# A decoder layer on one core: the mean-square matmul one block later with the next weight halves ahead of the normalisation, the last projection in 256 columns, the norm weight ahead of the scaling

## The chip, the cores and the metric

One Trainium2 chip, one of its cores. A core has a matrix engine (PE, with PEld for its weight loads), a vector engine (DVE), a scalar engine (ACT), GpSimd (POOL) and a sync engine (SP) that here issues nearly all DMAs. Each engine runs its own instructions in the order in which the program holds them, and waits for the others through semaphores. The metric is the device time of one execution in microseconds; lower is better.

## The reference

A decoder layer on 256 tokens of width 1024: a first SwiGLU feed-forward block, a mixer (a Mamba-2 branch beside a retention branch), a second feed-forward block, and a final norm. Nine vectors computed from a conditioning vector shift, scale and gate the three blocks. All is float32. Cut to what the change touches:

```python
def modulate(x, shift, scale):
    return x * (1.0 + scale[:, None, :]) + shift[:, None, :]

def swiglu(x, w_in, w_out):
    gate, up = jnp.split(x @ w_in, 2, axis=-1)
    return (jax.nn.silu(gate) * up) @ w_out

u = modulate(rms_norm(h, norm_ffn1_w[l]), sh1, sc1)
h = h + 0.5 * g1[:, None, :] * swiglu(u, ffn1_w_in[l], ffn1_w_out[l])
u = modulate(rms_norm(h, norm_mix_w[l]), sh2, sc2)
h = h + g2[:, None, :] * hybrid_mixer(u, ...)      # starts with u @ mix_w_in
u = modulate(rms_norm(h, norm_ffn2_w[l]), sh3, sc3)
h = h + 0.5 * g3[:, None, :] * swiglu(u, ffn2_w_in[l], ffn2_w_out[l])
return rms_norm(h, norm_final_w)
```

## The kernel before

Activations lie transposed, features on the partitions and the 256 tokens (`T`) along the row. Each float32 matrix product is done as three fast matmuls: both operands are split into a high half (rounded, float32r) and a low half (the rest), and `mm3` adds high x high, high x low and low x high into one bank (lines 143 to 151). Weights come by DMA in tiles of 2048 words (`wst`, four buffers). `half` turns 1024 words of one into a pair (`wh`, four buffers): ACT casts the high half, DVE subtracts it to get the low half. `HALVES_AT` says at which words of the buffer the two halves start. `pair_project` is the usual projection: a load, two such conversions, 48 matmuls of 256 columns with the weights stationary and u (tiles `uh` and `ul`) moving.

At two places, ahead of the mixer and ahead of the second feed-forward block, `modulated` hides the normalisation. The residual step leaves the unnormalised, scaled tiles in `nT` (or `s`) and in u. `early_project` projects these into four banks, in eight blocks of 12 matmuls (one for each of the eight feature tiles, `kt`), with two extra columns that carry the shift, so 258 columns. Between the blocks stands the mean-square matmul of `rstd` (line 217, two float32 matmuls of two passes each). ACT and DVE turn its result into the factor `rs`, then, for each of the eight tiles, DVE multiplies by `rs` (line 263), ACT writes the high half of the true u (line 234) and DVE the low half (line 235). Each u tile may only be overwritten when its early block is done. At the end the early banks are scaled by `rs` (lines 267 and 268).

What follows differs. In the mixer it is the dt tile, 16 short matmuls with a weight tile of its own (`dt_tile`: its halves are split by lines 140 and 141), then `conv.8`, a `pair_project` at columns `C_XS + 8 * 256`. In the second feed-forward block it is the gate half of the second pair, a `pair_project` at column 256. Nothing in these parts has an order written out by hand: a scheduler puts each engine's instructions into one order when the program is built, from its own estimate of when each could run.

The last projection (`ffn2_w_out`) is turned round: activations are stationary (`ah`, `al`), weights move. It runs over three blocks of output columns, 512, 256 and 256 wide; in each, for every one of 22 feature tiles and two row tiles, three matmuls. Behind each block come the gate (`gb`), the residual (`hN`), a square with its sum (`ss`) for the final norm and, but for the last block, the norm weight (`wf`). Behind the last, for each row tile, a square root, a reciprocal, the scaling and the DMAs to the output.

Of the kernel before, what the change touches and what calls it, by code (L numbers as in the profile page):

```python
# [12 lines left out]
F32 = mybir.dt.float32  # L13
# [5 lines left out]
P = 128  # L19
# [17 lines left out]
N_VEC = 344  # L37

U_ROW = 320
HALVES_AT = {"still": (6, 1056), "alike": (48, 1072), "moved": (26, 1088)}  # L40

K_ID, K_TRI, K_M = 0, 128, 256
K_INV, K_SGN = 384, 385
# [37 lines left out]
def layer(ctx: ExitStack, tc: tile.TileContext, a, out, packing):  # L81
# [71 lines left out]
    def at(pair, *idx):  # L153
        return pair[0][idx], pair[1][idx]
# [99 lines left out]
        dve.scalar_tensor_tensor(am, modc[:, jsc, :], 1.0, col[:, vn:vn + KD], ALU.add, ALU.mult)  # L254
        return am

    def modulated(ha, u, jsh, w, cols):
        rs = []
        ps = early_project(w, cols, u, 1, lambda: rs.append(rstd(sums, mean_m)))
        rs = rs[0]  # L260
        for f in range(KD):
            t = ha(f)
            dve.tensor_tensor(t, t, rs, ALU.mult)
            u_tile(u, f, t, jsh)
        b = sp.tile([P, 4], F32, tag="eb", name=nm("eb"), bufs=1)
        for i in range(4):
            dve.tensor_copy(b[:, i:i + 1], ps[i][:, T:T + 1])
            dve.tensor_tensor(ps[i][:, :T], ps[i][:, :T], rs, ALU.mult)
        return [(ps[i][:, :T], b[:, i:i + 1]) for i in range(4)]

    def early_project(w, cols, u, at_kt, between):
        sts = [load(w, 0, KD, c0, 256) for c0 in cols]
# [209 lines left out]
    with tc.tile_pool(name=nm("fp"), bufs=1, reuse_waits="tile") as fp:  # L482
# [41 lines left out]
        while ada_todo[0][0] in (2, 4):  # L524
# [1 line left out]
        am = scale_col(V_N2, 4)  # L526
        contract("ffn1_w_out", NF, lambda kt: (ah[:, kt, :], alo[:, kt, :]),
                 residual(2, 0.5, am, lambda f: nT[:, f, :], u, 3), lambda: ada_next(3, 5))
        first = modulated(lambda f: nT[:, f, :], u, 3, "mix_w_in", (C_Z, C_Z + 256))
    with tc.tile_pool(name="mx", bufs=1, reuse_waits="tile") as mx:  # L530
        def slot(shape, dt=F32, name="s"):
            return mx.tile(shape, dt, tag="slot", name=nm(name), bufs=SLOTS)
# [15 lines left out]
        rows = dp.tile([2, NH, P], F32, name="rows")  # L548

        def conv_pair(f0, dst):  # L550
            ps = pair_project(w_in, C_XS + f0 * P, u)
            t = mx.tile([P, 2, T], F32, tag="cv", name=nm("cv"), bufs=2)
            for f in range(2):
                def wc(tap):
                    i = V_CW + tap * 24 + f0 + f
                    return col[:, i:i + 1]
                act.activation(t[:, f, :], ps[:, f, :], AF.Identity,
                               bias=col[:, V_CB + f0 + f:V_CB + f0 + f + 1], scale=wc(3))
                for sh in (1, 2, 3):
                    dve.scalar_tensor_tensor(t[:, f, sh:], ps[:, f, :T - sh], wc(3 - sh),  # L560
                                             t[:, f, sh:], ALU.mult, ALU.add)
            lookup(dst, t, AF.Silu)
# [376 lines left out]
        def ha(f):  # L939
            return hA[f // 4][:, f % 4, :]  # L940
        contract("mix_w_out", 8, lambda kt: at(mh[kt // 4], al, kt % 4),
                 residual(5, 1.0, am, ha, u, 6), lambda: ada_next(6))
        first = modulated(ha, u, 6, "ffn2_w_in", (0, FFN))
    table("silu_and_others")
    with tc.tile_pool(name=nm("fp"), bufs=1, reuse_waits="tile") as fp:
        ah, alo = (fp.tile([P, NF * T + n], F32R, name=nm(name))[:, n:]
                   .rearrange("p (f t) -> p f t", f=NF) for name, n in (("ah", 0), ("al", 0)))
        w1 = "ffn2_w_in"
        hN = fp.tile([P, 2, D], F32, name="hN")
        gb = fp.tile([P, D], F32, name="gb")  # L950
# [1 line left out]
        for p2 in range(NF // 2):  # L952
            if p2 == 0:
                s = fp.tile([P, 2, T], F32, tag="s", name=nm("s"), bufs=2)
                for f in range(2):
                    lookup(s[:, f, :], first[f][0], AF.Silu, bias=first[f][1])
                    dve.scalar_tensor_tensor(s[:, f, :], first[2 + f][0], first[2 + f][1],
                                             s[:, f, :], ALU.add, ALU.mult)
                split_into(ah[:, 0:2, :], alo[:, 0:2, :], s)
            else:  # L960
                pg = pair_project(w1, p2 * 256, u)
                pu = pair_project(w1, FFN + p2 * 256, u)
                swiglu(fp, pg, pu, ah, alo, 2 * p2)
            ada_next()
            if p2 == 1:
                nc.sync.dma_start(wf, a["norm_final_w"].broadcast_to([P, D]))
            if p2 == 5:
                g = sp.tile([P, KD], F32, tag="g", name=nm("g"), bufs=2)
                dve.tensor_scalar(g, modc[:, 8, :], 0.5, None, ALU.mult)
                diag = fp.tile([P, KD, P], F32, tag="diag", name="diag")  # L970
                dve.tensor_tensor(diag, ident.unsqueeze(1).broadcast_to([P, KD, P]),
                                  g.unsqueeze(2).broadcast_to([P, KD, P]), ALU.mult)
                for q in range(2):
                    ps = misc_ps()
                    pe.matmul(ps, ones, diag[:, 4 * q:4 * q + 4, :].rearrange("p f t -> p (f t)"),  # L975
                              start=True, stop=True)
                    act.copy(gb[:, q * 512:(q + 1) * 512], ps)
            if p2 == 6:
                for tt in range(2):
                    for q in range(2):  # L980
                        ps = misc_ps()
                        for f in range(4):
                            pe.transpose(ps[:, f * P:(f + 1) * P],  # L983
                                         h[:, q * 4 + f, tt * P:(tt + 1) * P], ident)
                        act.copy(hN[:, tt, q * 512:(q + 1) * 512], ps)
# [3 lines left out]
        for bi, (c0, n) in enumerate(blocks):  # L989
# [4 lines left out]
            for k0 in range(0, NF, per):  # L994
                kn = min(per, NF - k0)
                st = load("ffn2_w_out", k0 * P, kn, c0, n)
                hvs = [half(st[:, k2:min(k2 + per // 2, kn), :],
                            "moved" if n == 256 else "alike") for k2 in range(0, kn, per // 2)]
                order = [(kk, tt) for kk in range(kn) for tt in range(2)]
                if final and k0 + kn == NF:  # L1000
                    order = [(kk, tt) for tt in range(2) for kk in range(kn)]
                for kk, tt in order:
                    kt, ts = k0 + kk, slice(tt * P, (tt + 1) * P)
                    mm3(ps[tt], (ah[:, kt, ts], alo[:, kt, ts]),
                        at(hvs[kk // (per // 2)], al, kk % (per // 2)), kt == 0, kt == NF - 1,
                        turned=n == 256 and tt == 0 and kt % 4 == 2)
            for tt in range(2):
                t = fp.tile([P, 512], F32, tag="t", name=nm("t"), bufs=2)[:, :n]
                o = hN[:, tt, cs_]
                dve.tensor_tensor(t, ps[tt], gb[:, cs_], ALU.mult)  # L1010
                dve.tensor_tensor(o, o, t, ALU.add)
                act.activation(t, o, AF.Square, accum_out=ss[:, tt, bi:bi + 1])
                if not final:
                    dve.tensor_tensor(o, o, wf[:, cs_], ALU.mult)
                if bi == 1:
                    s3 = ss[:, tt, 3:4]
                    dve.tensor_tensor(s3, ss[:, tt, 0:1], ss[:, tt, 1:2], ALU.add)
# [1 line left out]
                if final:  # L1019
# [1 line left out]
                    lookup(r, r, AF.Sqrt, bias=ss[:, tt, 3:4], scale=1.0 / D)  # L1021
                    dve.reciprocal(r, r)
                    rows = slice(tt * P, (tt + 1) * P)
                    lo_, mid = hN[:, tt, :512], hN[:, tt, 512:768]
                    if tt == 0:
                        act.activation(mid, mid, AF.Copy, scale=r)
                    else:
                        dve.tensor_scalar(mid, mid, r, None, ALU.mult)
                    dve.scalar_tensor_tensor(o, o, r, wf[:, cs_], ALU.mult, ALU.mult)
                    nc.sync.dma_start(out[rows, 512:], hN[:, tt, 512:])  # L1030
                    act.activation(lo_, lo_, AF.Copy, scale=r)
                    (act if tt else nc.sync).dma_start(out[rows, :512], lo_)


_SHAPES = {
# [39 lines left out]
```

## Time and profile before

| | us |
|---|---|
| three timed runs | 836.59, 839.97, 839.66 (median 839.66) |
| the profiled execution | 839.59 |
| its span in the trace | 836.8 |
| mean granted clock of PE | 0.998 of full speed |
| busy ACT, DVE | 515.6, 664.5 |

The page gives for each engine its busy time and share of the span, and lists of waits with what released them. A row of the timeline has a start in us from the span's start, the length in us, the engine, the line of the program, the operation, what it writes and reads, and how many such instructions in a row it stands for. On PE a matmul's end is modelled, so its pace is read from starts.

### The profile page before, as it was taken

What the parts mean: (1) busy time and instruction counts of PE and PEld (TensorE: products, weight loads), DVE (VectorE), ACT (ScalarE), POOL (GpSimd) and SP (SyncE); (2) the same over time, 40 slices, a digit from 0 to 9 for tenths busy, and PEclk for the clock granted to TensorE, in tenths of its full rate; (3) what the DMA queues carried; (4) which work ended last, traced back from release to release, by engine and by line L of the source; (5) the groups of instructions that cost most, each with busy time, mean ns of one, the idle gap of its engine ahead of it and who ended that gap; (6) DMA issues with size and microseconds to landing.
All of it is one profiled execution on the core that took longest, in us unless ns stands there. A gap on an engine that the chain in (4) does not pass through costs nothing. (4 is left out here: it accounts for less than half of the span.)

```text
span 836.8 us, 16156 instructions
## 1 busy us (share of the span) xinstructions
PE 821.9 (98%) x6734; PEld 795.6 (95%) x6734; DVE 664.5 (79%) x1002; ACT 515.6 (62%) x743; POOL 10.3 (1%) x21
## 2 busy tenths in 40 slices
PE   7999999999999999999999999999999999999996
PEld 6999999999999989999999999999999999999896
DVE  5999879896989987788898778977979985455463
ACT  6665444365888687756565569765658654545342
POOL 0000000000110010000000000000000000000000
PEclk9999999999999999999999999999999999999999
DMA  9987779995595555546658664655555785455521
GB/s 365 413 349 271 289 291 331 340 363 193 186 319 202 201 201 179 180 159 227 219 197 302 235 219 151 207 197 169 221 198 200 264 334 197 156 202 176 188 89 50
DMA packets 30586, 193.13 MB, mean 231 GB/s; under 512 B 3489, under 2 KB 4129, under 8 KB 10034
## 3 DMA queue, kind: packets, MB, share of 16 engines
q1 hardware_dynamic: 28656, 186.40, 61.0%
q0 software_dynamic: 1568, 5.28, 2.0%
q8 instruction: 52, 0.85, 0.4%
q10 hardware_dynamic: 290, 0.44, 0.1%
q14 instruction: 20, 0.16, 0.0%
HBM read 191.02 MB, written 1.08 MB: 230 GB/s over the span
## 5 line engine op out<-in xcount | busy, mean ns | idle before, releaser
L136 DVE TENSOR_TENSOR wh<-wst,wh 128x1024 fp32r<-128x1024 f32 (+1 forms) x263 | 316.6, 1208 | 103.7 <-ACT wh L135 102.7
L135 ACT CAST wh<-wst 128x1024 fp32r<-128x1024 f32 (+1 forms) x263 | 271.8, 1038 | 169.2 <-PE proj L151 115.3
L149 PE MATMUL proj<-uh,wh 128*128 128x256 f32 (+1 forms) x1160 | 322.2, 278 | 0.0
L150 PE MATMUL proj<-ul,wh 128*128 128x256 f32 (+1 forms) x1160 | 321.7, 277 | 0.0
L151 PE MATMUL proj<-uh,wh 128*128 128x256 f32 (+1 forms) x1160 | 321.3, 277 | 0.0
L150 PEld LDWEIGHTS proj<-ul,wh 128*128 128x128 f32 x1160 | 217.8, 188 | 0.9 <-issue 0.2
L151 PEld LDWEIGHTS proj<-uh,wh 128*128 128x128 f32 x1160 | 217.8, 188 | 0.5 <-DVE wh L404 0.2
L149 PEld LDWEIGHTS proj<-uh,wh 128*128 128x128 f32 x1160 | 217.9, 188 | 0.3 <-ACT wh L135 0.2
L149 PE MATMUL proj<-s,wh 128*128 128x256 f32 x312 | 86.9, 280 | 0.3 <-ACT s L140 0.3
L150 PE MATMUL proj<-s,wh 128*128 128x256 f32 x312 | 86.3, 277 | 0.0
L151 PE MATMUL proj<-s,wh 128*128 128x256 f32 x312 | 86.2, 277 | 0.0
L193 DVE SCALAR_TENSOR_TENSOR wst<-wst,cb 128x1024 f32<-128x1024 f32 x56 | 67.1, 1220 | 9.7 <-DMA wst<-in_ada_w_dram 9.2
L149 PEld LDWEIGHTS proj<-s,wh 128*128 128x128 f32 x312 | 58.4, 188 | 0.7 <-ACT s L140 0.5
L150 PEld LDWEIGHTS proj<-s,wh 128*128 128x128 f32 x312 | 58.5, 188 | 0.3 <-issue 0.2
L151 PEld LDWEIGHTS proj<-s,wh 128*128 128x128 f32 x312 | 58.6, 188 | 0.0
L151 PE MATMUL proj<-ah,wh 128*128 128x256 f32 x152 | 42.5, 279 | 1.6 <-DVE wh L136 1.6
L149 PE MATMUL proj<-ah,wh 128*128 128x256 f32 x152 | 42.1, 277 | 0.0
L150 PE MATMUL proj<-al,wh 128*128 128x256 f32 x152 | 42.0, 276 | 0.0
L145 PE MATMUL proj<-uh,wh 128*128 128x256 f32 x152 | 42.0, 276 | 0.0
L146 PE MATMUL proj<-uh,wh 128*128 128x256 f32 x152 | 42.0, 276 | 0.0
L147 PE MATMUL proj<-ul,wh 128*128 128x256 f32 x152 | 42.0, 276 | 0.0
L173 ACT ACT_TABLE_LOAD x30 | 38.5, 1283 | 1.2 <-PEq L1048 0.7
(271 smaller groups left out, 1370.2 us busy)
## 6 DMA issues: line engine op xcount, KB each, us to landing
wst<-in_mix_w_in_dram SPq DMA_DIRECT2D x52, 1024.0 KB, 4.9
wst<-in_ffn_w_in_dram SPq DMA_DIRECT2D x43, 1024.0 KB, 5.5
wst<-in_ada_w_dram SPq DMA_DIRECT2D x28, 1024.0 KB, 6.2
wst<-in_ffn_w_out_dram SPq DMA_DIRECT2D x17, 1024.0 KB, 5.5
ada<-in_ada_w_dram SPq DMA_DIRECT2D x16, 512.0 KB, 12.5
wst<-in_w_br_ssd_dram SPq DMA_DIRECT2D x8, 1024.0 KB, 5.5
wst<-in_w_br_ret_dram SPq DMA_DIRECT2D x8, 1024.0 KB, 4.8
wst<-in_ffn_w_out_dram SPq DMA_DIRECT2D x6, 768.0 KB, 5.9
```

Of the source, the lines that this page charges most:

```text
L135: act.copy(hi, v)
L136: dve.tensor_tensor(lo, v, hi.bitcast(F32), ALU.subtract)
L145: pe.matmul(o, l[1], r[0], start=False, stop=False, skip_group_check=skip)
L146: pe.matmul(o, l[0], r[0], start=False, stop=False, skip_group_check=skip)
L147: pe.matmul(o, l[0], r[1], start=False, stop=False, skip_group_check=skip)
L149: pe.matmul(o, l[0], r[0], start=first, stop=False, skip_group_check=skip)
L150: pe.matmul(o, l[0], r[1], start=False, stop=False, skip_group_check=skip)
L151: pe.matmul(o, l[1], r[0], start=False, stop=last, skip_group_check=skip)
L173: ins = act.preload_act_table_set(name).ins
L193: dve.scalar_tensor_tensor(st[:, i, :], st[:, i, :], 1.0, cb, ALU.mult, ALU.mult, accum_out=raw[:, j, f0 + i:f0 + i + 1])
```

## The change

Three parts.

1. `modulated` calls `rstd` ahead of the third block of the early projection and not of the second. Behind it, and ahead of the normalisation, it now loads and converts the weights of the next projection (`pair_halves`), and hands the two pairs to `conv.8` or to the second pair of the feed-forward block, which no longer make them.
2. In the last projection the 512-wide block is done as two matmuls of 256 columns each into the two parts of the bank. All three blocks use the same places for the halves, with the low half at word 1050, 1024 behind the high one. The tile of the low activations begins 26 words (104 bytes) later.
3. The norm weight is multiplied in at once for every block, ahead of the square root and the reciprocal; the square is written to a tile of its own. Behind the last block the first row tile is scaled in one piece of 1024 columns and goes out in one DMA of 512 KB; the second is scaled in two pieces of 512.

```diff
-HALVES_AT = {"still": (6, 1056), "alike": (48, 1072), "moved": (26, 1088)}
+HALVES_AT = {"still": (6, 1056), "alike": (48, 1072), "moved": (26, 1050)}
...
-    def modulated(ha, u, jsh, w, cols):
+    def modulated(ha, u, jsh, w, cols, c_next):
         rs = []
-        ps = early_project(w, cols, u, 1, lambda: rs.append(rstd(sums, mean_m)))
+        ps = early_project(w, cols, u, 2, lambda: rs.append(rstd(sums, mean_m)))
         rs = rs[0]
+        ready = pair_halves(w, c_next)
         for f in range(KD):
             t = ha(f)
             dve.tensor_tensor(t, t, rs, ALU.mult)
...
-        return [(ps[i][:, :T], b[:, i:i + 1]) for i in range(4)]
+        return [(ps[i][:, :T], b[:, i:i + 1]) for i in range(4)], ready
...
-        first = modulated(lambda f: nT[:, f, :], u, 3, "mix_w_in", (C_Z, C_Z + 256))
+        first, ready = modulated(lambda f: nT[:, f, :], u, 3, "mix_w_in", (C_Z, C_Z + 256),
+                                 C_XS + 8 * 256)
...
-            ps = pair_project(w_in, C_XS + f0 * P, u)
+            ps = pair_project(w_in, C_XS + f0 * P, u, ready if f0 == 16 else None)
...
-        first = modulated(ha, u, 6, "ffn2_w_in", (0, FFN))
+        first, ready = modulated(ha, u, 6, "ffn2_w_in", (0, FFN), 256)
...
-                   .rearrange("p (f t) -> p f t", f=NF) for name, n in (("ah", 0), ("al", 0)))
+                   .rearrange("p (f t) -> p f t", f=NF) for name, n in (("ah", 0), ("al", 26)))
...
-                pg = pair_project(w1, p2 * 256, u)
+                pg = pair_project(w1, p2 * 256, u, ready if p2 == 1 else None)
...
                 hvs = [half(st[:, k2:min(k2 + per // 2, kn), :],
-                            "moved" if n == 256 else "alike") for k2 in range(0, kn, per // 2)]
+                            "moved") for k2 in range(0, kn, per // 2)]
...
-                    mm3(ps[tt], (ah[:, kt, ts], alo[:, kt, ts]),
-                        at(hvs[kk // (per // 2)], al, kk % (per // 2)), kt == 0, kt == NF - 1,
-                        turned=n == 256 and tt == 0 and kt % 4 == 2)
+                    for d in range(n // T):
+                        mm3(ps[tt][:, d * T:(d + 1) * T], (ah[:, kt, ts], alo[:, kt, ts]),
+                            at(hvs[kk // (per // 2)], al, kk % (per // 2), slice(d * T, (d + 1) * T)),
+                            kt == d == 0, kt == NF - 1 and d == n // T - 1, skip=True,
+                            turned=tt == d == 0 and kt % 4 == 2)
...
-                dve.tensor_tensor(o, o, t, ALU.add)
-                act.activation(t, o, AF.Square, accum_out=ss[:, tt, bi:bi + 1])
-                if not final:
-                    dve.tensor_tensor(o, o, wf[:, cs_], ALU.mult)
+                dve.tensor_tensor(t, o, t, ALU.add)
+                q = fp.tile([P, 512], F32, tag="q", name=nm("q"), bufs=1)[:, :n]
+                act.activation(q, t, AF.Square, accum_out=ss[:, tt, bi:bi + 1])
+                dve.tensor_tensor(o, t, wf[:, cs_], ALU.mult)
...
-                    lo_, mid = hN[:, tt, :512], hN[:, tt, 512:768]
+                    lo_, up = hN[:, tt, :512], hN[:, tt, 512:]
                     if tt == 0:
-                        act.activation(mid, mid, AF.Copy, scale=r)
+                        act.activation(hN[:, 0, :], hN[:, 0, :], AF.Copy, scale=r)
+                        nc.sync.dma_start(out[rows, :], hN[:, 0, :])
                     else:
-                        dve.tensor_scalar(mid, mid, r, None, ALU.mult)
-                    dve.scalar_tensor_tensor(o, o, r, wf[:, cs_], ALU.mult, ALU.mult)
-                    nc.sync.dma_start(out[rows, 512:], hN[:, tt, 512:])
-                    act.activation(lo_, lo_, AF.Copy, scale=r)
-                    (act if tt else nc.sync).dma_start(out[rows, :512], lo_)
+                        dve.tensor_scalar(up, up, r, None, ALU.mult)
+                        nc.sync.dma_start(out[rows, 512:], up)
+                        act.activation(lo_, lo_, AF.Copy, scale=r)
+                        act.dma_start(out[rows, :512], lo_)
```

What the scheduler makes of the first part is seen in the order of the instructions. First DVE, ahead of the mixer, from the first normalised tiles on (`nT`); `wh_2537` is the weight tile of the dt tile, `wh_2623` belongs to conv.8. Before:

```order
L263 TENSOR_TENSOR nT<-nT,rs_2390 128x256 x3
L235 SCALAR_TENSOR_TENSOR ul_147<-nT,modc,uh_146 128x256 x3
L263 TENSOR_TENSOR nT<-nT,rs_2390 128x256 x4
L235 SCALAR_TENSOR_TENSOR ul_147<-nT,modc,uh_146 128x256 x2
L263 TENSOR_TENSOR nT<-nT,rs_2390 128x256
L141 TENSOR_TENSOR wh_2537<-wst_2535,wh_2537 128x8x32
L136 TENSOR_TENSOR wh_2623<-wst_2620,wh_2623 128x1024
L235 SCALAR_TENSOR_TENSOR ul_147<-nT,modc,uh_146 128x256
```

The same place with the change; `wh_2490` and `wh_2493` are the two pairs of conv.8, `wh_2545` is the dt tile's, and the rows left out are copies and scalings of the early banks:

```order
L264 TENSOR_TENSOR nT<-nT,rs_2402 128x256 x3
L136 TENSOR_TENSOR wh_2490<-wst_2488,wh_2490 128x1024
L136 TENSOR_TENSOR wh_2493<-wst_2488,wh_2493 128x1024
L235 SCALAR_TENSOR_TENSOR ul_147<-nT,modc,uh_146 128x256 x3
L264 TENSOR_TENSOR nT<-nT,rs_2402 128x256 x3
L235 SCALAR_TENSOR_TENSOR ul_147<-nT,modc,uh_146 128x256 x3
L264 TENSOR_TENSOR nT<-nT,rs_2402 128x256 x2
...
L235 SCALAR_TENSOR_TENSOR ul_147<-nT,modc,uh_146 128x256 x2
L269 TENSOR_TENSOR misc_2367<-misc_2367,rs_2402 128x256
L268 COPY eb_2520<-misc_2368 128x1
L141 TENSOR_TENSOR wh_2545<-wst_2543,wh_2545 128x8x32
```

Both low halves of conv.8 moved up between the tiles and the low u's, and the dt half moved from behind the fifth low u to behind the last. On ACT the high half of the dt tile moved in the same way, from behind the third high u to behind the sixth, and into another buffer, the one that the early projection reads last.

On PE the order around the dt tile is as it was. With the change, from the last matmul of the early projection on (a bracket names the engines that an instruction waits for):

```order
L151 MATMUL misc_2368<-uh_146,wh_2437 128x258
L588 MATMUL proj_2548<-uh_146,wh_2545 64x256 [waits DVE_49,Activation_49]
L590 MATMUL proj_2548<-ul_147,wh_2545 32x256
L587 MATMUL proj_2548<-ul_147,wh_2545 32x256
L588 MATMUL proj_2548<-uh_146,wh_2545 64x256
```

The dt tile still comes first; the matmuls of conv.8, whose halves are now made ahead, stand behind its sixteen. In the second feed-forward block the two pairs moved up on DVE in the same way, and there the projection that reads them follows the early one directly.

Last, the start of the last projection on PE. Before:

```order
L149 MATMUL proj_8978<-wh_8982,ah_7722 128x512
L150 MATMUL proj_8978<-wh_8982,ah_7722 128x512
L151 MATMUL proj_8978<-wh_8982,al_7723 128x512
L149 MATMUL proj_8979<-wh_8982,ah_7722 128x512
L150 MATMUL proj_8979<-wh_8982,ah_7722 128x512
L151 MATMUL proj_8979<-wh_8982,al_7723 128x512
```

With the change:

```order
L149 MATMUL proj_8978<-wh_8982,ah_7730 128x256
L150 MATMUL proj_8978<-wh_8982,ah_7730 128x256
L151 MATMUL proj_8978<-wh_8982,al_7731 128x256
L149 MATMUL proj_8978<-wh_8982,ah_7730 128x256
L150 MATMUL proj_8978<-wh_8982,ah_7730 128x256
L151 MATMUL proj_8978<-wh_8982,al_7731 128x256
```

Each group of three for one bank has become two groups of three, one for each part of its columns.

## The prediction, written before the changed kernel ran

> **What bounds the kernel now.** I read the head of the page first, then the list of what the matrix engine (PE) waited for, then the pace of its matmuls.
>
> ```profile
> span 836.8 us, 16156 instructions
> PE 821.9 (98%) x6734; PEld 795.6 (95%) x6734; DVE 664.5 (79%) x1002; ACT 515.6 (62%) x743; POOL 10.3 (1%) x21
> ```
> ```profile
> PE misc L380 <- DMA crow<-in_c_dram: 3.0, 1, 3.0
> PE proj L151 <- DVE wh L136: 1.6, 3, 0.8
> ...
> PE misc L217 <- ACT sq L246: 0.9, 1, 0.9
> ```
>
> PE is busy for 98% of the span and the whole list of its waits holds a handful of microseconds, 3.0 of them at the start. So nothing but PE sets the time: a change gains what it takes off PE's own stream, and loses whatever it makes PE wait. DVE, at 79%, is the one to watch, because PE is fed by it. The third row is the only listed wait that the change aims at.
>
> The pace of a matmul is read from starts, since its recorded end is a model.
>
> ```profile
> 720.00:750.00 30.00, 30.00 (x266) 1.00 0.51 178
> ```
> ```profile
> 768.05 0.40 PE L149 MATMUL proj<-wh,ah 128*128 128x512 f32 x1
> ...
> 797.99 0.28 PE L149 MATMUL proj<-wh,ah 128*128 128x256 f32 x1
> ...
> 829.43 0.28 PE L151 MATMUL proj<-wh,al 128*128 128x256 f32 x1
> ```
>
> The first row is a stretch of 256-column matmuls with weights stationary (columns: window, its length, PE busy with the count, granted clock, DMA share, GB/s): 266 in 30.00 us, 112.8 ns each. The last projection has 22 x 2 x 3 = 132 matmuls of 512 columns from 768.05 to 797.99, 226.8 ns each, that is 113.4 per 256 columns. Then come 264 of 256 columns up to 829.43: 31.44 us over 263 intervals, 119.5 ns each.
>
> **Part 1, first place: the mixer's normalisation.** The mean-square matmul (L217) moves from behind one block of the early projection (12 matmuls) to behind two.
>
> ```profile
> 201.45 0.60 PE L217 MATMUL misc<-ssum,k 128*128 128x256 f32 x2
> 202.06 0.70 PE L217 MATMUL misc<-sq,k 128*128 128x256 f32 x2
> 202.41 0.47 PE L149 MATMUL proj<-uh,wh 128*128 128x258 f32 x1
> 202.72 0.28 PE L150 MATMUL proj<-ul,wh 128*128 128x258 f32 x1
> ...
> 212.62 0.28 PE L586 MATMUL proj<-uh,wh 128*64 128x256 f32 x1
> ```
>
> From 202.72 to 212.62 PE does 83 matmuls, 0.119 us each, so a block takes 1.43. L217 now starts at 201.45 + 1.43 = 202.88. It takes between 0.6 (0.25 for the first pair, as in the second place below, plus 0.35 for the second) and the 0.96 of now; I take 0.8. PE gains about 0.2 and reaches the dt tile at 212.4 instead of 212.62.
>
> What follows is on ACT and DVE.
>
> ```profile
> 202.80 0.48 ACT L181 ACTIVATE rs<-misc,epsc 128x256 f32<-128x256 f32 x1
> ...
> 205.47 1.10 DVE L263 TENSOR_TENSOR nT<-nT,rs 128x256 f32<-128x256 f32 x3
> 206.48 1.27 DVE L235 SCALAR_TENSOR_TENSOR ul<-nT,modc,uh 128x256 fp32r<-128x256 f32 x3
> 207.67 1.42 DVE L263 TENSOR_TENSOR nT<-nT,rs 128x256 f32<-128x256 f32 x4
> ...
> 210.14 0.42 DVE L141 TENSOR_TENSOR wh<-wst,wh 128x256 fp32r<-128x256 f32 x1
> 210.47 1.22 DVE L136 TENSOR_TENSOR wh<-wst,wh 128x1024 fp32r<-128x1024 f32 x1
> 211.61 0.48 DVE L235 SCALAR_TENSOR_TENSOR ul<-nT,modc,uh 128x256 fp32r<-128x256 f32 x1
> ...
> 212.87 0.21 DVE L267 COPY eb<-misc 128x1 f32<-128x1 f32 x2
> 213.00 0.42 DVE L268 TENSOR_TENSOR proj<-proj,rs 128x256 f32<-128x256 f32 x1
> 213.33 0.42 DVE L268 TENSOR_TENSOR misc<-misc,rs 128x256 f32<-128x256 f32 x1
> ```
>
> The rstd chain began 0.74 after the second pair started (202.06 to 202.80) and gave the first normalised tile its start at 205.47. With the second pair at about 203.3 the chain begins at 204.05, and the first tile starts at 206.7.
>
> Now the order on DVE, shown above, decides. Before, the low half of the dt weights (210.14) stood after 8 tiles and 5 low u's, and ended at 210.56, two microseconds ahead of PE. In the change it stands behind 8 tiles, 8 low u's, both low halves of the conversion brought forward, three of the four scalings of the early banks, and the copies. From start to start these cost: a tile 0.34 (205.47 to 206.48 for three), a low u 0.40 (206.48 to 207.67), a half 1.14 (210.47 to 211.61), a scaling 0.33 (213.00 to 213.33), a copy 0.07. The sum is 8 x 0.34 + 8 x 0.40 + 2 x 1.14 + 3 x 0.33 + 4 x 0.07 = 9.5, and 0.42 for the dt half itself: 206.7 + 9.9 = 216.6. Its high half is no way out: it takes the buffer that the early projection reads to its end, and stands behind six high u's on ACT.
>
> PE's next instruction in order is the first dt matmul, which waits for both halves. Behind it in the same queue stands the whole convolution projection, ready or not. So **PE stands from 212.5 to 216.6**, and the dt tile starts 4.0 us later than before. The bounds: 3.4 if DVE waits nowhere and L217 is short, 5.0 if the high halves (ACT, freed by PE at about 206) hold DVE too. What stands behind the dt tile may give some back, since ACT and DVE work on during the pause; the list names no wait of PE there, so this is an estimate, 0.4, between 0 and 0.8. First place: **+3.6**.
>
> **Part 1, second place: the last FFN.** Here the wait is real.
>
> ```profile
> 643.50 0.60 PE L217 MATMUL misc<-ssum,k 128*128 128x256 f32 x2
> 643.75 0.47 PE L149 MATMUL proj<-uh,wh 128*128 128x258 f32 x1
> ...
> 645.86 0.28 PE L149 MATMUL proj<-uh,wh 128*128 128x258 f32 x1
> ...
> 655.51 0.28 PE L149 MATMUL proj<-uh,wh 128*128 128x256 f32 x1
> ```
> ```profile
> 656.93 0.47 DVE L235 SCALAR_TENSOR_TENSOR ul<-s,modc,uh 128x256 fp32r<-128x256 f32 x1
> ```
>
> From 643.50 to 645.86 PE does L217 and three matmuls. Without a wait that is 0.8 + 0.31 + 2 x 0.12 = 1.35, so 1.0 is gained (0.86 by the list at least), and the next projection could start at 654.5 instead of 655.51. No dt tile stands between, and the same work stands ahead of the last low u, so that one moves only with rs, by 0.2, to an end of about 657.6. Its reader is the 23rd matmul of the projection, at 654.5 + 22 x 0.114 = 657.0, so 0.6 goes back into a wait for u. Second place: **-0.4**, between -1.0 and +0.3.
>
> The two moved weight loads go ahead of a dt load and of an ada load on the SP queue; the list names a single wait of PE for a DMA, the one at the start, and I cost them at nothing. If a load came late, a conversion behind it on ACT would be late by as much.
>
> **Part 2: the last projection.** Its 132 matmuls of 512 become 264 of 256, and the low half starts exactly 1024 words behind the high one (1062 before in the 256-column blocks). The fast forms above read moving tiles that lie a multiple of 128 bytes apart (u's halves; the 512-column halves, 1024 words apart); the form at 119.5 is the one that doesn't. The changed layout has that property and, with the low activations 104 bytes on, the same differences to the stationary tile as the fast 256-column form. I take 113.4 for all 528: 59.9 against 29.94 + 31.56 = 61.5, **-1.6**. The bounds: 112.8 gives -1.9; 119.5 for all gives +1.6.
>
> The Trainium skill ("TensorE: Matmul & The Clock Gate", section "Back-to-back issue gap") gives a fixed 2.5 ns per matmul beside its columns. By it the split would add 132 x 2.5 ns = 0.33 us, an estimate; the trace has 113.4 for half a 512 and 112.8 for a 256, and no such fixed part.
>
> **Part 3: the tail.**
>
> ```profile
> 829.65 0.48 DVE L1029 SCALAR_TENSOR_TENSOR hN<-hN,ss,wf 128x256 f32<-128x256 f32 x1
> 830.06 0.42 DVE L1010 TENSOR_TENSOR t<-proj,gb 128x256 f32<-128x256 f32 x1
> 830.07 0.71 ACT L1031 ACTIVATE hN<-hN,ss 128x512 f32<-128x512 f32 x1
> ...
> 830.97 0.42 ACT L1012 ACTIVATE t<-hN 128x256 f32<-128x256 f32 x1 [0.19 <-DVE hN L1011]
> ...
> 832.81 0.33 SPq L1030 DMA_DIRECT2D out_dram<-hN  x1
> ```
>
> The norm-weight product of the first row tile no longer stands ahead of the second one's first step (830.06), which may start 0.3 earlier. But ACT now scales 1024 columns in one piece, about 0.71 + 0.42 = 1.1 from 829.65, and the second square (830.97) starts at 830.75, 0.2 earlier. The last DMA goes 0.2 to 0.4 earlier, against a first output of 512 KB that leaves 0.6 later and may still be moving. I take **-0.2**, between -0.5 and +0.5.
>
> **The sum:** 3.6 - 0.4 - 1.6 - 0.2 = +1.4. The profiled execution took 839.59 (span 836.8 and 2.8 around it), 0.07 under the median of 839.66, so no correction is needed: 839.59 + 1.4 = **841.0 us**.
>
> **The rivals.**
>
> *The dt tile is not held up.* If DVE ran the dt half early after all, as at 210.14 before, the first place would be -0.2: 839.59 - 0.2 - 0.4 - 1.6 - 0.2 = 837.2. For it speaks only that the pause does not exist now; against it speaks a fixed order on DVE and on PE. A part of it (buffers freed earlier) is in my bound of 3.4. Chance 0.10.
>
> *The pause costs PE its clock.* This one ends clearly slower.
>
> ```profile
> 834.30:836.80 2.50, 0.00 (x0) 0.00 (x0) 0.00 (x0) 0.00 (x0) 0.00 (x0) 0.50 0.29 111
> ```
>
> After the last matmul (829.43, ended 829.7) the granted clock is at 0.50 by 834.3, 4.6 us later. The forecast pause is 4.1 long, so it is near that point: from some 4.6 us on at this phase, earlier at another, the following matmuls run at half pace. One to two stretches of some 3.4 us at half pace cost 1.7 to 3.4, so 843.5. Nothing else in the trace pauses so long after the start. Chance 0.18. The Trainium skill (same page, section "What's actually happening") says that the clock falls after an idle window of about 3.4 us, of windows that run freely; by it a pause of 4.1 would hold a whole window in about (4.1 - 3.4) / 3.4 = 0.2 of executions, an estimate, and the fall after 829.7 agrees with it.
>
> *The split keeps the uneven pace.* If the 119.5 comes from the short moving read of the weights and not from the offsets, 528 matmuls take 63.1: 841.0 + 3.2 = 844.2. For it: no 256-column matmul with moving weights runs at 113 now. Against it: the 512 form with moving weights does. Chance 0.11.
>
> **How the numbers follow.** Forecast 0.59, the rivals 0.10, 0.18 and 0.11, 0.02 for the rest. The range reaches from the first rival to the third, with the bounds of the terms: 837.0 to 844.4. Half a per cent, about what a measurement of this kernel can tell from no change, is 4.2 us. All gains at their ends (0.36 + 1.05 + 1.9 + 0.5, no pause) give 835.8, so faster by that much needs luck: 0.04. Slower by that much takes most of the third rival, part of the second, or both: 0.13. The rest, 0.83, is in between.
>
> **What would show it.** In the changed profile: L217 in both places with no wait for ACT; a PE wait of 3.4 to 5.0 us at the dt tile at about 212, named as a wait for DVE or as an idle stretch, with the granted clock beside it; the low u's as the releaser of a short wait behind the second early projection; 528 matmuls in some 59.9 us; the last output DMA some 3.2 us after the last matmul. I am wrong if PE passes the dt tile without a pause, or if the last projection takes over 61.5.

## The result, and the profile after

| | median of 6, us | lowest to highest | profiled execution | its span |
|---|---|---|---|---|
| before | 839.11 | 836.59 to 841.22 | 839.59 | 836.8 |
| after | 845.82 | 844.74 to 847.89 | 847.89 | 846.1 |

The ratio is 1.0092, with a 95% interval of 1.0076 to 1.0108: 6.7 us slower, where 1.4 slower was forecast in a range that ended at 844.4. The forecast was wrong. The profiled execution of after is the longest of its six; its span is 9.3 us above that of before, and this is what the trace has to account for.

The head of the page after the change, and PE's list of waits (engine, line, what it waited for; total, times, longest):

```profile
span 846.1 us, 16410 instructions
...
PE 827.6 (98%) x6866; PEld 806.6 (95%) x6866; DVE 664.6 (79%) x1002; ACT 516.0 (61%) x742; POOL 10.3 (1%) x21
```
```profile
PE proj L588 <- DVE wh L141: 4.1, 1, 4.1
...
PE proj L150 <- DVE ul L235: 0.3, 1, 0.3
```

The wait for the mean square's last square (0.9 before) is gone, and a wait of 4.1 for the dt tile's low half has come, both as forecast. But PE is busy for 5.7 us more than before, and no list of waits shows that. The timeline at the dt tile (columns: start, length, engine, line, operation, what it writes and reads, shape, count, idle time before it with its releaser):

```profile
212.87 0.29 PE L151 MATMUL misc<-uh,wh 128*128 128x258 f32 x1
...
216.68 0.41 DVE L141 TENSOR_TENSOR wh<-wst,wh 128x256 fp32r<-128x256 f32 x1
...
217.24 0.45 PE L588 MATMUL proj<-uh,wh 128*64 128x256 f32 x1 [4.08 <-DVE wh L141]
...
217.70 0.41 PE L587 MATMUL proj<-ul,wh 128*32 128x256 f32 x1
217.91 0.41 PE L588 MATMUL proj<-uh,wh 128*64 128x256 f32 x1
```

The dt half starts at 216.68, some 6.5 us later than before (210.14), and ends at 217.09; the forecast had it end at 216.6. Behind it the matmuls start 0.21 apart, where they start 0.11 apart at full clock. The windows of the same kernel tell more (columns: window, its length, busy time and count of PE, PEld, DVE, ACT and POOL, granted clock, DMA share, GB/s):

```profile
216.00:216.50 0.50, 0.00 (x0) 0.00 (x0) 0.50 (x2) 0.00 (x0) 0.00 (x0) 1.00 0.00 0
216.50:217.00 0.50, 0.00 (x0) 0.00 (x0) 0.50 (x3) 0.00 (x0) 0.00 (x0) 0.50 0.00 0
217.00:226.50 9.50, 9.26 (x42) 8.65 (x43) 5.14 (x16) 4.70 (x10) 0.00 (x0) 0.50 0.45 144
226.50:227.00 0.50, 0.50 (x5) 0.50 (x5) 0.43 (x3) 0.50 (x1) 0.00 (x0) 0.76 0.93 393
```

The granted clock falls to 0.50 at 216.50, in the pause, and comes back at 226.74 (a mean of 0.76 over the half microsecond from 226.50 means 0.24 us of it at 0.50). That is 10.24 us, of which PE works for more than nine. This is my second rival, at a larger price than the 1.7 to 3.4 that I gave it.

The last projection and the end, from the timeline:

```profile
776.05 0.28 PE L149 MATMUL proj<-wh,ah 128*128 128x256 f32 x1
...
839.24 0.28 PE L151 MATMUL proj<-wh,al 128*128 128x256 f32 x1
...
842.06 0.34 SPq L1034 DMA_DIRECT2D out_dram<-hN  x1
842.29 0.35 ACTq L1036 DMA_DIRECT2D out_dram<-hN  x1
```

The 528 matmuls take 63.19 us from the first start to the last, 119.9 ns each; before, from 768.05 to 829.43, it was 61.38. So my third rival has come true as well, and with it one of the signs of being wrong that the prediction named, a last projection of over 61.5. From the last matmul to the end of the span it is 6.86 us, against 7.37 (836.8 less 829.43).

To cut the span into parts I use four marks that both programs have: the first matmul of the early projection ahead of the mixer, the first transpose behind the mixer's first convolutions (L647 before, L649 after), the first matmul of the early projection ahead of the last feed-forward block, and the first of the last projection. Rows of before, then of after:

```profile
200.03 0.28 PE L149 MATMUL proj<-uh,wh 128*128 128x258 f32 x1
...
282.55 0.60 PE L647 MATMUL misc<-k,s 128*128 128x128 f32 x4
...
642.07 0.28 PE L149 MATMUL proj<-uh,wh 128*128 128x258 f32 x1
```
```profile
200.69 0.28 PE L149 MATMUL proj<-uh,wh 128*128 128x258 f32 x1
...
290.92 0.60 PE L649 MATMUL misc<-k,s 128*128 128x128 f32 x4
...
650.49 0.28 PE L149 MATMUL proj<-uh,wh 128*128 128x258 f32 x1
```

| stretch | before | after | difference | forecast |
|---|---|---|---|---|
| start to the mixer's early projection | 200.03 | 200.69 | +0.66 | 0 |
| first place, up to the first transpose | 82.52 | 90.23 | +7.71 | +3.6 |
| mixer | 359.52 | 359.57 | +0.05 | 0 |
| second place and feed-forward block | 125.98 | 125.56 | -0.42 | -0.4 |
| last projection | 61.38 | 63.19 | +1.81 | -1.6 |
| tail | 7.37 | 6.86 | -0.51 | -0.2 |
| span | 836.8 | 846.1 | +9.3 | +1.4 |

The first stretch holds the same instructions in both; none of the kernels below changes it either, and there this mark stands anywhere from 198.16 to 200.75, so the 0.66 is the spread between executions. The other stretches repeat far better: the first place takes 82.41 to 82.52 in the eight kernels that leave it as it was. Two rows are off: the first place by 4.1, the last projection by 3.4.

### The profile page after: what moved, and what is told of

It is laid out like the page before. It is cut to its first block, busy times and chain, and to the rows that moved or that the text cites. A ratio compares the mean times of both kernels' runs of the same rounds, so it can differ in the third digit from the quotient of the medians.

```text
span 846.1 us, 16410 instructions
## 1 busy us (share of the span) xinstructions
PE 827.6 (98%) x6866; PEld 806.6 (95%) x6866; DVE 664.6 (79%) x1002; ACT 516.0 (61%) x742; POOL 10.3 (1%) x21
## 5 line engine op out<-in xcount | busy, mean ns | idle before, releaser
L135 ACT CAST wh<-wst 128x1024 fp32r<-128x1024 f32 (+1 forms) x263 | 271.8, 1039 | 175.0 <-PE proj L151 112.8
L150 PE MATMUL proj<-wh,ah 128*128 128x256 f32 x161 | 45.5, 283 | 0.0
L149 PE MATMUL proj<-wh,ah 128*128 128x256 f32 x161 | 45.5, 282 | 0.0
L151 PE MATMUL proj<-wh,al 128*128 128x256 f32 x161 | 45.4, 282 | 0.0
```

Source lines behind the costliest of these rows:

```text
L135: act.copy(hi, v)
L149: pe.matmul(o, l[0], r[0], start=first, stop=False, skip_group_check=skip)
L150: pe.matmul(o, l[0], r[1], start=False, stop=False, skip_group_check=skip)
L151: pe.matmul(o, l[1], r[0], start=False, stop=last, skip_group_check=skip)
```

## The experiments

### The four parts, each alone

Each kernel is the one before with one part of the change.

```diff
+        first, ready = modulated(lambda f: nT[:, f, :], u, 3, "mix_w_in", (C_Z, C_Z + 256),
+                                 C_XS + 8 * 256, 2)      # mixer_place; the other place as before
...
+        first, ready = modulated(ha, u, 6, "ffn2_w_in", (0, FFN), 256, 2)      # ffn2_place
```

The numbers at the ends of the calls are the first column of the weights converted ahead, and the block ahead of which `rstd` is called. `last_proj` has the diff's lines from `hvs` to `turned` with the two offsets, `tail` those behind them.

> The kernel before with the change at the mixer's normalisation alone. Theory (pause and clock): PE stands some 4.2 us ahead of the first dt matmul, then runs at a granted clock of 0.50 for some 9 us, which costs it half of that again: 3.9 + 4.5 = +8.4 in an execution where the clock falls so, and +5 to +8.5 in the median. Rival (pause alone): the clock is no part of it, +3.5 to +4.2 and granted 1.00 all through 210 to 230.

> The kernel before with the change at the last FFN's normalisation alone. Theory: the wait of the mean-square matmul (0.9) goes, some 0.6 of it comes back as a wait for the low u's, the clock stays at 1.00: -0.4, between -1.0 and +0.3. Rival (this place pauses and loses clock as the mixer's does): +4 or more. Rival (nothing is gained): 0.

> The kernel before with the last projection's new layout alone (256 columns throughout, high half 104 bytes on, low half 1024 words behind it). Theory (the layout itself is slow): all 528 matmuls go at 119 to 120 ns, 63.2 us against 61.5: +1.5 to +1.9. Rival (the pace is a consequence of what the other parts do): 113.4 ns, 59.9 us, -1.6.

> The kernel before with the new tail alone. Theory: the end comes some 0.5 us sooner after the last matmul (6.9 us from its start to the end of the span, against 7.4): -0.5. Rival (the single output DMA of 512 KB holds the end): 0 to +0.5.

| | median, us | before beside it | ratio, 95% interval |
|---|---|---|---|
| mixer_place | 843.75 (6) | 838.61 (29) | 1.0065 [1.0047, 1.0083] |
| ffn2_place | 838.96 (11) | 838.61 | 1.0004 [0.9994, 1.0014] |
| last_proj | 840.73 (11) | 838.61 | 1.0030 [1.0019, 1.0040] |
| tail | 837.95 (11) | 838.61 | 0.9992 [0.9981, 1.0002] |

The medians differ by +5.1, +0.4, +2.1 and -0.7; their sum, 6.9, is close to the whole change's 6.7. So nothing shows that the parts work on each other, within the microsecond or so that these medians can tell, and two of them carry the loss. The clock of the mixer's part alone, by windows:

```profile
212.00:214.50 2.50, 0.00 (x0) 0.00 (x0) 2.50 (x11) 2.50 (x7) 0.00 (x0) 1.00 0.61 256
214.50:215.00 0.50, 0.00 (x0) 0.00 (x0) 0.50 (x2) 0.20 (x2) 0.00 (x0) 0.88 0.00 0
215.00:225.00 10.00, 8.95 (x40) 8.35 (x41) 5.69 (x18) 4.42 (x9) 0.00 (x0) 0.50 0.40 125
225.00:225.50 0.50, 0.50 (x6) 0.50 (x5) 0.43 (x3) 0.48 (x2) 0.00 (x0) 0.88 0.93 360
```

It is low from 214.88 to 225.12, again 10.24 us. The layout of the last projection is slow by itself: in `last_proj` it takes 63.19 us (767.68 to 830.87), as in the whole change, against the rival by which other parts cause it. `ffn2_place` takes 125.56 us for its stretch (642.61 to 768.17), the same -0.42 as in the whole change; in the median so little cannot be seen.

### The pause without the clock

PE is kept at work in the pause by matmuls that nobody reads.

```diff
             split_into(wd[:, :, :NH], wd[:, :, NH:], st)
+            warm(16)      # mixer_filled; 8 in mixer_half_filled
             ps = proj_ps()
             for kt in range(KD):
```

`warm(n)` is the kernel's own helper: n matmuls of ones by ones into a bank of `pm`.

> The change at the mixer alone, with 16 matmuls of ones by ones (128 columns, float32) put on PE ahead of the dt tile, whose result nobody reads. They keep PE at work for some 3.5 of the 4.3 us in which it stands there. Theory (the pause costs the clock in about half of the executions, 3 windows of 3.4 us at half pace when it does): dt starts when it did, the granted clock stays at 1.00, and every execution is +3.8 to +4.3 over the kernel before, with no second cluster at +7 to +8 as the change at the mixer alone has. Rival (the half pace after the pause has another cause): +5.1 in the median and 214 ns a matmul again from 216 to 225.

> The change at the mixer alone, with 8 matmuls of ones by ones ahead of the dt tile instead of 16: PE stands for some 2.6 us instead of 4.3. Theory (the clock falls only after a whole window of some 3.4 us without work): granted 1.00 throughout, +3.5 to +4.3 as with 16. Rival (a pause of 2.6 is enough): the clock falls in some executions, 214 ns a matmul behind the pause, and the median lies a microsecond higher.

> The change at the mixer alone once more, beside the kernel with 8 matmuls in its pause, to bound what the clock costs in the median. Theory (it falls in about half of the executions, at 4 to 4.5 us each): +4.5 to +6.5, 1 to 2.5 over the filled kernel; the profiled execution has either three windows at 0.50 or none. Rival (it falls every time): +7.5 to +8.5.

The dt tile starts 4.3 to 4.4 us behind the early projection in all of them. What follows is read between the first two marks, in rows of `mixer_filled`:

```profile
198.16 0.28 PE L149 MATMUL proj<-uh,wh 128*128 128x258 f32 x1
...
210.47 3.73 PE L368 MATMUL misc<-ones 128*128 128x128 f32 x32
214.70 0.30 PE L589 MATMUL proj<-uh,wh 128*64 128x256 f32 x1 [0.50 <-DVE wh L141]
...
284.31 0.60 PE L650 MATMUL misc<-k,s 128*128 128x128 f32 x4
```

| | marks | between them | over before | clock at 0.50 | median over the kernel before |
|---|---|---|---|---|---|
| mixer_filled | 198.16, 284.31 | 86.15 | +3.6 | none | +4.2, 1.0049 [1.0031, 1.0067] |
| mixer_half_filled | 199.18, 286.88 | 87.70 | +5.2 | 3.4 us | +5.1, 1.0057 [1.0040, 1.0074] |
| mixer_place_again | 198.25, 285.77 | 87.52 | +5.0 | 3.4 us | +4.8, 1.0060 [1.0041, 1.0079] |
| mixer_place | 199.51, 289.55 | 90.04 | +7.5 | 10.2 us | +5.1 |
| the whole change | 200.69, 290.92 | 90.23 | +7.7 | 10.2 us | |

With the pause filled the same lateness costs 3.6 us, and the clock does the rest: 1.4 to 1.6 where it is low for 3.4 us, 3.9 to 4.1 where it is low for 10.2. Two expectations missed in part: the six executions of `mixer_filled` lie from 840.47 to 844.67, much wider than +3.8 to +4.3 (those of the kernel before, from 835.84 to 841.30, are as wide), and the profiled execution of `mixer_place_again` has one low stretch of 3.4 us, not three or none. The theory by which the clock needs a whole window without work falls with `mixer_half_filled`. Its pause and clock, from the timeline and the windows:

```profile
211.48 1.95 PE L368 MATMUL misc<-ones 128*128 128x128 f32 x16
215.71 0.36 PE L589 MATMUL proj<-uh,wh 128*64 128x256 f32 x1 [2.28 <-DVE wh L141]
```
```profile
215.00:216.00 1.00, 0.29 (x2) 0.29 (x3) 1.00 (x6) 0.00 (x0) 0.00 (x0) 0.91 0.00 0
216.00:219.00 3.00, 3.00 (x16) 2.70 (x15) 1.13 (x1) 0.00 (x0) 0.00 (x0) 0.50 0.74 232
219.00:220.00 1.00, 1.00 (x9) 0.85 (x7) 0.00 (x0) 0.69 (x2) 0.00 (x0) 0.88 0.84 352
```

PE stood for 2.28 us, and the clock still fell, at 215.82, just after work had begun again; it came back at 219.24, 3.42 us later. In `mixer_place_again` it fell 0.74 us after the dt tile's first matmul (214.78):

```profile
212.00:215.00 3.00, 0.22 (x2) 0.24 (x3) 3.00 (x14) 1.44 (x5) 0.00 (x0) 1.00 0.10 41
215.00:216.00 1.00, 1.00 (x9) 0.93 (x8) 1.00 (x2) 0.00 (x0) 0.00 (x0) 0.76 0.39 82
216.00:218.00 2.00, 2.00 (x11) 1.87 (x10) 0.20 (x1) 0.15 (x1) 0.00 (x0) 0.50 0.86 336
218.00:219.00 1.00, 1.00 (x7) 0.78 (x5) 0.00 (x0) 1.00 (x2) 0.00 (x0) 0.53 0.70 295
```

It was low from 215.52 to 218.94. In all four profiled executions with a pause of 2.3 us or more at the dt tile the clock fell there, and in none of the others. The medians tell less: the four intervals overlap, and the clock's share in them, 0.6 to 0.9 by the differences to `mixer_filled`, is smaller than in any of these traces. The mean granted clock is measured in every execution, and says how often it falls at all:

| | mean granted clock of the executions |
|---|---|
| the kernel before, beside these runs | 0.997 to 0.999 in all |
| mixer_filled | 0.997 to 0.999 in all six |
| mixer_half_filled | 0.993 to 0.996 in four, 0.998 in two |
| mixer_place and mixer_place_again | 0.991 to 0.996 in all twelve |
| the whole change | 0.993 in three, 0.997 in three |

The profiled executions give the scale: 0.996 with one low stretch of 3.4 us, 0.991 and 0.993 with 10.2 us. The kernels without the pause have 0.996 in two executions of all (one of `even_256`, one of `wide_512`) and 0.997 to 0.999 in the others. So with the pause unfilled the clock fell in eight of the twelve executions and very likely in the other four, which show 0.996; with it filled it fell in none that can be told. At 0.997 one low stretch can't be told from none, so in three executions of the whole change it stays open. Why an execution gets one such stretch or three is not shown.

### What makes the pause: the late mean square or the halves brought forward

```diff
+        first, ready = modulated(lambda f: nT[:, f, :], u, 3, "mix_w_in", (C_Z, C_Z + 256),
+                                 None, 2)
```

> The change at the mixer alone, with the mean-square matmul behind two blocks but without the convolution's weight halves ahead of the normalisation. On DVE the dt tile's low half then stands behind 8 tiles and 6 low u's, without the two conversions. Theory (the halves brought forward make the pause): it ends some 5.5 us after the first tile starts, within 0.3 us of PE; what is left is a wait of some 0.4 for the last low u and of up to 1 for the convolution's halves, +0.5 to +1.8, granted 1.00. Rival (the later mean square makes it): a pause of over 3, +3.5 or more.

The median is 838.44 (12 executions) against 838.54, with a ratio of 1.0007 [0.9995, 1.0019], and the stretch between the marks (199.99 to 282.76) is 0.25 longer. DVE's part of the timeline, and the one wait of PE that is listed there:

```profile
206.57 2.10 DVE L264 TENSOR_TENSOR nT<-nT,rs 128x256 f32<-128x256 f32 x6
208.59 2.47 DVE L235 SCALAR_TENSOR_TENSOR ul<-nT,modc,uh 128x256 fp32r<-128x256 f32 x6
210.97 0.76 DVE L264 TENSOR_TENSOR nT<-nT,rs 128x256 f32<-128x256 f32 x2
211.64 0.42 DVE L141 TENSOR_TENSOR wh<-wst,wh 128x256 fp32r<-128x256 f32 x1
...
215.36 0.39 PE L151 MATMUL proj<-uh,wh 128*128 128x256 f32 x1 [0.54 <-DVE wh L136]
```

The dt half starts 5.07 behind the first tile, and PE, which is done with the early projection at about 212.3, has it. A rstd that is one block later costs next to nothing here, 0.25 in the trace where +0.5 to +1.8 was expected; with the two conversions in front of the normalisation the pause is there, because they push the dt half behind the last u tiles and the scalings. Whether they would make it with the mean square where it was before was not tried. The wait for the convolution's halves was bounded at 1 and measured 0.54.

### What sets the pace of the last projection

```diff
-                            "moved" if n == 256 else "alike") for k2 in range(0, kn, per // 2)]
+                            "alike") for k2 in range(0, kn, per // 2)]      # even_256
...
-                   .rearrange("p (f t) -> p f t", f=NF) for name, n in (("ah", 0), ("al", 0)))
+                   .rearrange("p (f t) -> p f t", f=NF) for name, n in (("ah", 22), ("al", 16)))
```

The second pair of lines is added in `even_256_phase`.

> The kernel before, with the weight halves of its two 256-column blocks laid where those of the 512-column block lie (192 bytes on, low half 1024 words behind). Theory (where a moving row starts sets the pace: every matmul at 113 to 114 ns starts its moving rows at 32 modulo 128 bytes, every one at 119 to 120 at 72 or 96): the 264 matmuls go at 113.4 instead of 119.5, -1.6. Rival (256 columns of weights are a slow read wherever they lie): 0.

> As the run before, with the activations moved too (high 88 bytes on, low 64), so that stationary and moving tiles both lie modulo 128 bytes as in the matmuls at 113 to 114 ns. Theory (the moving start alone): the same -1.6. Rival (the stationary tile must lie away from the moving one): -1.6 here and 0 in the run before. Rival (256 columns of weights are slow wherever they lie): 0 in both.

Medians of 838.44 and 838.99 (11 each) against 838.54, both ratios 1.0004, [0.9991, 1.0018] and [0.9991, 1.0016]: nothing gained. Where the weight halves lie does not set the pace. In `even_256` the 256-column matmuls begin at 796.97, when the offsets are those of the 512-column ones just before:

```profile
796.97 0.28 PE L149 MATMUL proj<-wh,ah 128*128 128x256 f32 x1
...
828.52 0.28 PE L151 MATMUL proj<-wh,al 128*128 128x256 f32 x1
```

That is 31.55 us for 263 intervals, 120.0 ns each. Moving the activations did harm elsewhere: the projection took 62.03 us (769.00 to 831.03) instead of the 61.50 of `even_256` (767.02 to 828.52). By their starts the 512-column matmuls went from 226.9 to 233.3 ns, and the 256-column ones from 120.0 to 118.8. The groups by form show it at the 512-column matmuls, whose mean (a modelled length, last number but one) was 389 in `even_256`:

```profile
L151 PE MATMUL proj<-wh,al 128*128 128x512 f32 x44 | 17.5, 398 | 0.0
L149 PE MATMUL proj<-wh,ah 128*128 128x512 f32 x44 | 17.4, 395 | 0.0
```

Then the columns of a matmul are what is left: two blocks of 512, first with the tail of before, then with the changed one.

```diff
-        blocks = ((0, 512), (512, 256), (768, 256))
+        blocks = ((0, 512), (512, 512))
...
-                if bi == 1:
+                if bi == 0:
                     s3 = ss[:, tt, 3:4]
-                    dve.tensor_tensor(s3, ss[:, tt, 0:1], ss[:, tt, 1:2], ALU.add)
-                    dve.tensor_scalar(s3, s3, 1.0 / D, EPS, ALU.mult, ALU.add)
+                    dve.tensor_scalar(s3, ss[:, tt, 0:1], 1.0 / D, EPS, ALU.mult, ALU.add)
```

> The kernel before with the last projection in two blocks of 512 columns instead of one of 512 and two of 256. Theory (a matmul with weights moving has a fixed part of some 13.3 ns beside its columns, so 264 matmuls are cheaper than 528): 264 x 226.8 = 59.9 us for the projection against 61.5, -1.6; its last steps work on 512 columns each instead of 256, +0.8 to +1.0 at the end: -0.6 to -0.8 in all. Rival (the pace of the second half of the columns has another cause, such as what ACT and DVE do then): 240 ns a matmul there again, +0.8 to +1.0.

> The run before with the changed kernel's tail, the two parts that should each gain: -1.6 for the projection, -0.5 to -0.7 for the tail, +0.8 for the longer last steps: -1.3, about 837.3, faster than both kernels. Rival (the tail's gain is lost where its last block is 512 wide): -0.6.

The projection and the end of `wide_512`:

```profile
766.38 0.40 PE L149 MATMUL proj<-wh,ah 128*128 128x512 f32 x1
...
826.02 0.39 PE L151 MATMUL proj<-wh,al 128*128 128x512 f32 x1
...
830.39 0.38 ACTq L1027 DMA_DIRECT2D out_dram<-hN  x1
830.42 0.33 SPq L1025 DMA_DIRECT2D out_dram<-hN  x1
```

The projection takes 59.64 us over 263 intervals, 226.8 ns a matmul and 1.74 us less than before; from the last matmul to the end of the span (834.5) it is 8.5 us instead of 7.4, which takes two thirds of it back. The median is 837.27 (12) against 838.14 (23), the ratio 0.9993 [0.9982, 1.0003]. With the changed tail it is 837.50, and 0.9986 [0.9975, 0.9997]: faster than before by 1.2 us by the ratio, and the only version here whose interval excludes no gain. It beats both kernels, by little. The tail's gain is lost in it, as the rival had it: its projection takes 59.64 us too, and it is 8.7 us from the last matmul to the end of the span, not 8.5. Rows of `wide_512_tail`:

```profile
827.17 0.39 PE L151 MATMUL proj<-wh,al 128*128 128x512 f32 x1
...
828.99 1.15 ACT L1025 ACTIVATE hN<-hN,ss 128x1024 f32<-128x1024 f32 x1 [0.25 <-DVE ss L1021]
...
830.05 0.61 ACT L1013 ACTIVATE q<-t 128x512 f32<-128x512 f32 x1
```

The second square stands on ACT behind the scaling of 1024 columns and starts 2.9 us behind the last matmul; in `wide_512` it is 1.9 (827.89).

## Why the prediction was wrong, point by point

- **PE's pause at the dt tile: right, in place, cause and size.** The forecast was a pause from 212.5 to 216.6, a dt tile 4.0 later than before, 0.4 given back behind it, and +3.6 net. The pause came from some 213.0 to 217.24. On DVE the dt half starts 9.40 behind the first tile (207.28 to 216.68), where the sum had 9.5. Counted from the first mark the dt tile starts 3.96 later (16.55 against 12.59), and with the clock kept the stretch lost 3.6, so some 0.3 came back.
- **The pause costs PE its clock: called a rival at 0.18 and left out of the sum; it was the rule.** What failed is the point "from some 4.6 us on at this phase". I took it from the end of the kernel, where the clock fell some 4.6 us after the last matmul. That shows that so much idle time is enough, and says nothing of how much is needed. Here 4.1 us were enough in eight of the twelve executions with this part alone and very likely in the other four, and 2.3 in four of six. The price was mis-sized too: 1.4 to 4.1 in the traces, not 1.7 to 3.4, since the low clock lasts 3.4 or 10.2 us; in the medians of the part alone it is no more than 0.9.
- **The last projection: the step that failed outright.** "I take 113.4 for all 528", with the argument that the slow form is the one whose halves lie an uneven distance apart. The rows quoted allowed another reading: 226.8 ns for 512 columns and 119.5 for 256 lie on a line with a slope of 0.42 ns a column and a fixed part of some 12 ns. Halving a matmul adds one more fixed part: 132 x (2 x 119.9 - 226.8) = 1.7 us, and +1.81 was measured. I had divided the 512-column time by two and compared it with a 256-column form whose weights are stationary, another kind of matmul. `even_256` shows that the offsets of the weight halves do nothing, `wide_512` that the columns do.
- **The second place: right.** -0.42 against -0.4: the wait went, and 0.3 of it came back as a listed wait for the low u's (at 665.49, the 20th matmul of the projection, where the 23rd was forecast), with some 0.3 more around it.
- **The tail: right in sign, too small in size.** -0.5 against -0.2, at the edge of its bounds; the median of the part alone has -0.7, with an interval that just reaches no change.

Put together with the measured sizes: 839.59 + 3.6 - 0.4 + 1.8 - 0.5 is 844.1 without the clock, and 845.5 to 848.2 with it. Five of the six executions lie from 845.17 to 847.89. The sixth, at 844.74, lies below that range although its granted clock is 0.993, so executions differ by as much as the clock costs. Each of the two rivals was priced as if it came alone; the range covered each alone, and not both together.

The Trainium skill bears on both failed steps. The Trainium skill ("TensorE: Matmul & The Clock Gate", section "What's actually happening") has the clock fall after an idle window of about 3.4 us, windows running freely, and come back after a busy one. The length agrees with the traces (3.42 and three times 3.41). That a window must be idle does not: it fell with 0.7 to 1.1 us of work in the 3.4 us ahead of it (212.10 to 215.52, and 212.40 to 215.82), and the chance of 0.2 that I worked out from the rule was far too low. That one busy window brings it back agrees with two of the four low phases, and not with the two of 10.24 us. And the fixed 2.5 ns per matmul of the Trainium skill's section "Back-to-back issue gap", which I set aside because the trace had "no such fixed part", had the right sign; the trace's own figure for this form is some 13 ns.

## What to carry to other kernels

Before splitting or merging matmuls, fit a line through two widths of the same form (same operand moving, same stationary) and price the fixed part; never compare per-column paces of different forms. A forecast pause of PE of two microseconds or more (2.3 was enough here) is priced twice, once as the pause and once as the work behind it at half pace. Filling it with matmuls that nobody reads took the second price away here, with a wait of 0.5 us left; filling half of it did not. When work is brought forward in front of a chain, look at what stands behind that chain on the same engine and is needed first.

## What the runs showed of the hardware

- The granted clock's low phases have lengths of 3.42, 3.42, 10.24 and 10.24 us. After two of the pauses one such stretch of work was enough to end it, after two others three were needed, though PE was busy all through the second (219.91 to 223.32 in the changed kernel). The long phases are the two whose fall came ahead of the dt tile (by 0.74 us in the changed kernel and 1.17 in `mixer_place`), the short ones those whose fall came behind its first matmul (by 0.74 and 0.11). What decides was not tried.
- In all 14 profiled executions the time between two changes of the granted clock is a whole number of 3.413 us: in the changed kernel 181 of them, 617.8 us, from 226.74 to the fall at 844.56. So where in such a stretch a pause lies may decide whether the clock falls, as in four executions of six with 2.3 us; no run varies that alone. 1.1 us of work in one did not hold the clock (`mixer_half_filled`); 2.3 us did in the kernel before, from 827.43 to 830.85, the stretch ahead of the idle one that ends with its fall at 834.26.
- A matmul of float32r halves costs, beside its columns, about 13 ns with weights moving (226.8 at 512, 119.9 at 256) and about 6 with weights stationary (112.8 at 256, if a column costs the same 0.42 ns there). Neither the places of the weight halves nor, as far as tried, those of the activations explain the difference; it stays open.
- Starting the stationary activations 88 and 64 bytes later (`even_256_phase` against `even_256`, one profiled execution each) slows 512-column matmuls from 226.9 to 233.3 ns and the projection by 0.53 us, with nothing else changed.
